# Layer 1 of a two-layer decoder: one compressor input for both block halves, its key part moved ahead of the last keys, and scores of both query tiles issued together

## The chip, the cores and the metric

The kernel runs on one core of one Trainium2 chip. The metric is the device time of one execution in microseconds (us). "Before" is the median of three runs; the profile is of one more execution.

## What is computed

The reference is a decoder trunk of two layers on 256 tokens of width 1024 in fp32. Layer 0 mixes tokens by stick-breaking and differential attention, layer 1 by a sparse attention with three branches; each mixer is followed by an MLP of width 4096. The change touches the mixer of layer 1 alone. Cut to what matters there:

```
def compress(t, pos, w1, w2):          # t: 256 x 4 groups x 64; CMP_LEN 32, CMP_STRIDE 16
    chunks = t.reshape(B, 16, 16, G, Dh)
    blocks = concatenate([chunks[:, r:r + 15] for r in range(2)], axis=2) + pos
    return gelu(flat(blocks) @ w1) @ w2            # 15 blocks per group, flat width 32 * 64

def nsa_attention(...):                            # 16 heads in 4 groups, 256 queries in 2 tiles
    o_cmp = softmax(q kc^T - slope * distance) vc          # over the 15 compressed blocks
    o_sel = softmax(q ks^T - slope * distance) vs          # selected keys: all of the past here
    o_win = softmax(q kw^T - slope * distance) vw          # window keys: all of the past here
    return g0 * o_cmp + g1 * o_sel + g2 * o_win
```

A block of 32 tokens is two neighbouring chunks of 16. So the product with `w1` is one product for the first halves of the blocks (chunks 0 to 14) and one for the second halves (chunks 1 to 15).

## The kernel before

All projections are "split" products: each fp32 weight tile is cast to a high part by ScalarE (L66), its low part is subtracted out by VectorE (L69), and TensorE makes three products per 128 rows (high by high, high by low, low by high). `Weights` holds them: raw tiles come by DMA on SP's queue (4 half-tile buffers), split ones have 4 buffers, and `get` splits one tile ahead. The order of `weight_order` is the order in which they are taken.

`odd_mixer` writes the order of TensorE's work by hand. Its pieces are generators, and `run(a, b, ...)` interleaves their steps in proportion. A scheduling layer below then fixes every engine's queue and gives out the buffers. The pieces are:

- `keys("ks")`, `keys("kw")`: selected and window keys, 48 matmuls each (`ps_k`), copied to `kd` by ScalarE (L720) and VectorE (L721).
- `queries(g)`: 48 matmuls (`ps_q`) per group of four heads, evicted to `qs` by ScalarE (L950).
- `compress_blocks(kv)`: the compressor's input, keys (kv = 0) or values (kv = 1): 48 matmuls (`ps_c`), and a transposed position row (`ps_pos`). Copies on ScalarE (L877) and VectorE (L879) bring the result into two tiles `fsk` or `fsv`, one for the first and one for the second halves of the blocks: 8 copies on each engine, and a fill on GpSimd (L864). It also loads eight tiles of `w1` (`cwk`, `cwv`). All these tiles share one ring of 12 buffers (`small`), with the transposed probabilities `pT` of later.
- `compress_hidden(kv)`: 16 products `ps_h` of the `fs` and `cw` tiles; `compress_gelu`: copies `ps_h` out (`hc`, L897), transposes it and adds the position (`ps_hT`, by the matrix `fold`), and applies gelu on ScalarE and VectorE (L905 to L921); `compress_keys`, `compress_values`: the product with `w2` (`ps_co`).
- `nsa_scores(g, t, b)`: four products per group g, query tile t (128 keys for t = 0, 256 for t = 1) and branch b, into one of two PSUM buffers of the tag `s2`. VectorE then adds the distance and finds the extreme (L975), ScalarE exponentiates (L978), and GpSimd scales (L983). `nsa_cmp_scores(g)` (`sc`) takes one of the same two buffers.
- `nsa_transposes`, `nsa_products` (steps of `values`): transposes of the probabilities (`pt`), their copies `pT` on ScalarE and VectorE in turn (L1031, L1029), and the product with the values (`o`).

Apart from the scores, every PSUM result of these pieces takes one of four banks of the tag `B`, so a result that isn't copied out holds its bank. The hand-written order before is: keys ks, queries 0, keys kw with scores (0,0) between, compressor blocks of keys, then of values, half of queries 1, hidden of keys, the other half of queries 1, hidden of values, and so on.

## Time and profile before

| | |
|---|---|
| median of 3 runs | 662.26 us (661.87 to 663.5) |
| profiled execution | 662.43 us, its span 660.7 us |
| TensorE matmul busy | 641.3 us, 97% of the span |
| VectorE busy | 407.7 us |
| ScalarE busy | 345.5 us |
| GpSimd busy | 46.3 us |
| mean granted TensorE clock | 0.991 |

The span is the time from the first to the last instruction. The rest of the execution's time, 1.7 us, lies around it. A wait is put down to the releaser that came last. A matmul's row gives its start and the time until its result is out, which is longer than the distance to the next matmul's start, because matmuls overlap. An fp32 product of scores, transposes or the compressor shows as two records.

### The profile page before, as it was taken

The numbers are of one execution on the slowest core, as the hardware profiler recorded it, in microseconds if no ns is written. First come the engines' busy times: TensorE is split into PE (matmuls) and PEld (weight loads), VectorE is DVE, ScalarE is ACT, GpSimd is POOL, SyncE is SP. The second block draws the span as 40 slices with busy tenths as digits, with TensorE's granted clock in tenths as the row PEclk, the third lists the DMA queues.
The fourth block names the chain that finished last, engine by engine and source line by source line (L and its number), as shares of the span: only waits on it lengthen the run. The fifth ranks groups of instructions, "written<-read, shape, count | busy, mean of one in ns | idle before, by whom it ended". The sixth has DMA issues, their size and how long they took to land.

```text
span 660.7 us, 11136 instructions
## 1 busy us (share of the span) xinstructions
PE 641.3 (97%) x4257; PEld 562.2 (85%) x4257; DVE 407.7 (62%) x820; ACT 345.5 (52%) x699; POOL 46.3 (7%) x139
## 2 busy tenths in 40 slices
PE   6999999999999999999999899999999999999995
PEld 3799898899898989988899778777899898999984
DVE  4845577886555555555877476776765555555534
ACT  5564666464444444543567374654554444444523
POOL 2200000000000000000203231440000000000000
PEclk8899999999999999999999999999999999999999
DMA  6785243456565556664596612014365555555501
GB/s 253 226 257 157 73 176 106 156 183 208 178 182 182 186 188 192 191 191 141 173 307 208 223 64 64 23 43 156 118 214 186 182 183 181 188 189 189 192 2 64
DMA packets 74277, 108.67 MB, mean 164 GB/s; under 512 B 5072, under 2 KB 60400, under 8 KB 74224
## 3 DMA queue, kind: packets, MB, share of 16 engines
q1 hardware_dynamic: 74224, 107.97, 50.9%
q8 instruction: 33, 0.54, 0.3%
q14 instruction: 20, 0.16, 0.1%
HBM read 106.91 MB, written 1.05 MB: 163 GB/s over the span
## 4 chain that ended last, share of the span: by engine, by line
PE 90%; DVE 5%; ACT 2%; issue 1%; DMA 1%; SPq 0%; ACTq 0%; DVEq 0%
PE macc L108 27%; PE ps_up L108 24%; PE ps_f L108 7%; PE acc L108 5%; PE ps_q L108 4%; PE ps_ut L108 3%; PE ps_v L108 2%; PE o L108 2%; PE s L108 2%; PE ps_or L108 2%; PE ps_k L108 2%; PE pt L1026 2%; DVE wl L69 2%; PE z L108 1%; PE ps_h L108 1%
## 5 line engine op out<-in xcount | busy, mean ns | idle before, releaser
L69 DVE TENSOR_TENSOR wl<-w,wh 128x1024 fp32r<-128x1024 f32 (+1 forms) x188 | 224.9, 1214 | 166.1 <-ACT wh L66 165.6
L66 ACT CAST wh<-w 128x1024 fp32r<-128x1024 f32 (+1 forms) x190 | 192.9, 1040 | 172.7 <-PE macc L108 83.3
L108 PE MATMUL macc<-wh,l 128*128 128x512 f32 x256 | 101.2, 395 | 0.0
L108 PE MATMUL macc<-wh,h 128*128 128x512 f32 x256 | 101.1, 395 | 0.0
L108 PE MATMUL macc<-wl,h 128*128 128x512 f32 x256 | 101.0, 394 | 0.0
L108 PE MATMUL ps_up<-m0h,wh 128*128 128x256 f32 x224 | 63.5, 283 | 0.0
L108 PE MATMUL ps_up<-m1h,wh 128*128 128x256 f32 x224 | 63.5, 283 | 0.0
L108 PE MATMUL ps_up<-m0h,wl 128*128 128x256 f32 x224 | 63.4, 283 | 0.0
L108 PE MATMUL ps_up<-m1h,wl 128*128 128x256 f32 x224 | 63.3, 283 | 0.0
L108 PE MATMUL ps_up<-m1l,wh 128*128 128x256 f32 x224 | 63.3, 283 | 0.0
L108 PE MATMUL ps_up<-m0l,wh 128*128 128x256 f32 x224 | 63.3, 283 | 0.0
L108 PEld LDWEIGHTS macc<-wh,l 128*128 128x128 f32 x256 | 48.2, 188 | 11.1
L108 PEld LDWEIGHTS macc<-wh,h 128*128 128x128 f32 x256 | 48.4, 189 | 10.0
L108 PEld LDWEIGHTS macc<-wl,h 128*128 128x128 f32 x256 | 48.3, 189 | 10.0
L108 PEld LDWEIGHTS ps_up<-m0l,wh 128*128 128x128 f32 x224 | 42.9, 191 | 0.6
L108 PEld LDWEIGHTS ps_up<-m1l,wh 128*128 128x128 f32 x224 | 42.9, 191 | 0.6
L108 PEld LDWEIGHTS ps_up<-m1h,wh 128*128 128x128 f32 x224 | 42.9, 191 | 0.6
L108 PEld LDWEIGHTS ps_up<-m0h,wh 128*128 128x128 f32 x224 | 42.9, 191 | 0.6
L108 PEld LDWEIGHTS ps_up<-m1h,wl 128*128 128x128 f32 x224 | 42.9, 191 | 0.0
L108 PEld LDWEIGHTS ps_up<-m0h,wl 128*128 128x128 f32 x224 | 42.9, 191 | 0.0
L983 POOL TENSOR_SCALAR p<-p,sums 128x128 f32<-128x128 f32 (+1 forms) x64 | 31.4, 508 | 80.5 <-ACT kd L720 25.8
L108 PE MATMUL ps_f<-x0h,wh 128*128 128x256 f32 x128 | 36.5, 285 | 0.0
(285 smaller groups left out, 1191.2 us busy)
## 6 DMA issues: line engine op xcount, KB each, us to landing
w<-in_mlp_w_dram SPq DMA_DIRECT2D x128, 512.0 KB, 4.3
w<-in_ev_w_in_dram SPq DMA_DIRECT2D x24, 512.0 KB, 4.8
w<-in_od_w_in_dram SPq DMA_DIRECT2D x18, 512.0 KB, 5.0
w<-in_ev_w_out_dram SPq DMA_DIRECT2D x8, 512.0 KB, 4.3
w<-in_od_w_out_dram SPq DMA_DIRECT2D x8, 512.0 KB, 3.6
cwk<-in_od_cmp_k_w_dram SPq DMA_DIRECT2D x8, 256.0 KB, 6.5
cwv<-in_od_cmp_v_w_dram SPq DMA_DIRECT2D x8, 256.0 KB, 5.1
w<-in_od_w_in_dram SPq DMA_DIRECT2D x4, 304.0 KB, 2.9
```

Source lines behind the costliest of these rows:

```text
L66: self.nc.scalar.copy(wh[:, c], w)
L69: eng.tensor_sub(wl[:, c], w, wh[:, c].bitcast(F32))
L108: self.nc.tensor.matmul(out, lhsT, rhs, start=start, stop=stop, **kw)
L983: nc.gpsimd.tensor_scalar(o[:, h], o[:, h], sums[:, h : h + 1], 0.0, op0=ALU.mult, op1=ALU.add)
L1026: nc.tensor.transpose(pt[:, h * P : (h + 1) * P], p[g, t, b][:, h, kt * P : (kt + 1) * P], self.ident)
```

## The change

The input of the compressor is held in one tile `fs` of its own (66 columns per step: a position column, 64 chunk columns, a position column) and both halves of the blocks read it, shifted by two columns; it has 16 columns a group instead of 15, so the copies are 4 on each engine and each part, and GpSimd fills nothing. `fold` is moved to the new columns. The ring `small` has 11 buffers instead of 12. The compressor's key part (`compress_blocks(0)`) now stands ahead of the keys kw, its hidden product right behind them, and the value part follows; the loads are reordered to fit. The scores of the two query tiles are issued one behind the other, and their softmax behind both; in the `values` steps they follow the products.

```
@@ -229,8 +229,8 @@

         W.add(("ks",), cols(w, 1536, 256))
         q(0)
+        W.add(("c", 0), cols(w, 1024, 256))
         W.add(("kw",), cols(w, 2048, 256))
-        W.add(("c", 0), cols(w, 1024, 256))
         W.add(("c", 1), cols(w, 1280, 256))
         q(1)
         q(2)
@@ -730,67 +730,79 @@

             def scores(g, b):

-                yield 2
-                for t in range(2):
-                    self.nsa_scores(g, t, b, qs, kd, gates, p, up, banks)
+                todo = [self.nsa_scores(g, t, b, qs, kd, gates, p, up, banks) for t in range(2)]
+                for f in todo:
+                    next(f)
+                return todo
+
+            def cmp_scores(g):
+                todo = self.nsa_cmp_scores(g, qs, kd, gates, pc[g % 2], banks)
+                next(todo)
+                return [todo]
+
+            def soft(todo):
+                for f in todo:
+                    for _ in f:
+                        pass
+
+            def once(f, n=3):
+
+                yield n
+                for i in range(n):
+                    if i == n // 2:
+                        f()
                     yield 1

-            def cmp_scores(g):
-                self.nsa_cmp_scores(g, qs, kd, gates, pc[g % 2], banks)
-
             order = [(g, t) for g in range(NG) for t in range(2)]

-            def values(i):
+            def values(i, *scores):

                 g, t = order[i]
                 todo = self.nsa_transposes(g, t, p, pc[g % 2], parts, up)
                 yield next(todo)
                 for n, _ in enumerate(todo):
-                    if n == 0 and i > 0:
-                        products(i - 1)
+                    if n == 0:
+                        if i > 0:
+                            products(i - 1)
+                        for f in scores:
+                            soft(f())
                     yield 1

             def products(i):
                 g, t = order[i]
                 self.nsa_products(g, t, parts, oT, v2, vc)

+            f = [None, None]
             run(keys("ks", CW))
             run(queries(0))
-            run(keys("kw", CW + S), scores(0, 0))
-            f = [None, None]
-            run(self.compress_blocks(0, xT, up, pool, f), scores(0, 1))
-            run(self.compress_blocks(1, xT, up, pool, f))
-            q1 = queries(1)
-            next(q1)
-            run(part(q1, KT))
+            run(self.compress_blocks(0, xT, up, pool, f))
+            run(keys("kw", CW + S), once(lambda: soft(scores(0, 0))))
             h = [self.bankB(f"ps_h{kv}") for kv in range(2)]
             run(self.compress_hidden(f[0], h[0]))
             hk = self.compress_gelu(0, h[0], up)
-            run(part(q1, KT))
-            run(self.compress_hidden(f[1], h[1]), scores(1, 0))
+            run(self.compress_blocks(1, xT, up, pool, f))
+            run(queries(1), once(lambda: soft(scores(0, 1))))
+            run(self.compress_hidden(f[1], h[1]))
+            soft(scores(1, 0))
+            self.compress_keys(hk, f[0], kd)
             hv = self.compress_gelu(1, h[1], up)
-            self.compress_keys(hk, f[0], kd)
             q2 = queries(2)
             next(q2)
-            run(part(q2, KT), scores(1, 1))
+            run(part(q2, KT))
+            soft(cmp_scores(0))
+            soft(scores(1, 1))
             self.compress_values(hv, f[1], vc)
-            cmp_scores(0)
             run(part(q2, KT), values(0))
-            cmp_scores(1)
             q3 = queries(3)
             next(q3)


-            run(values(1), part(q3, 4))
-            run(values(2), part(q3, 6), scores(2, 0))
-            run(values(3), part(q3, 6), scores(2, 1))
-            cmp_scores(2)
+            run(values(1, lambda: cmp_scores(1)), part(q3, 4))
+            run(values(2, lambda: scores(2, 0)), part(q3, 6))
+            run(values(3, lambda: scores(2, 1)), part(q3, 6))
             rows = self.out_rows("odo", oT)
-            next(values4 := values(4))
-            run(part(values4, 1))
-            run(part(values4, 2), part(rows, 2), scores(3, 0))
-            run(values(5), part(rows, 2), scores(3, 1))
-            cmp_scores(3)
+            run(values(4, lambda: cmp_scores(2), lambda: scores(3, 0)), part(rows, 2))
+            run(values(5, lambda: cmp_scores(3), lambda: scores(3, 1)), part(rows, 2))
             run(values(6), part(rows, 2))
             run(values(7), part(rows, 2))
             products(7)
@@ -835,9 +847,10 @@
         return pool.tile(shape, F32, tag="p1", name=name, bufs=4)

     def small(self, pool, shape, name):
-        return pool.tile(shape, F32, tag="p2", name=name, bufs=12)
+        return pool.tile(shape, F32, tag="p2", name=name, bufs=11)

     def compress_blocks(self, kv, xT, up, pool, f):
+


         yield 2 * KT
@@ -857,26 +870,24 @@
                 w = self.small(up, [P, 2, S], f"cw{nm}{u}{hf}")
                 nc.sync.dma_start(w, w1[u, hf])
                 ws.append(w)
-        fs = [self.small(up, [P, 8, 64], f"fs{nm}{hf}") for hf in range(2)]
+        fs = up.tile([P, 8, 66], F32, tag="fs", name=f"fs{nm}", bufs=1)
         pp = self.bankB("ps_pos")
         nc.tensor.transpose(pp[:, :16], pos, self.ident[:16, :16])
         for hf in range(2):
-            nc.gpsimd.memset(fs[hf][:, :, 61:], 0.0)
-            nc.scalar.copy(fs[hf][:, :, 60], pp[:, 8 * hf : 8 * hf + 8])
+            nc.scalar.copy(fs[:, :, 65 * hf], pp[:, 8 * hf : 8 * hf + 8])
         w = self.W.get(("c", kv))
         for m in range(2):
             ps = self.bankB("ps_c")
             yield from self.fmajor_steps(ps[:, :S], w, m, xT)
             for i in range(2):
                 src = ps[64 * i : 64 * i + 64, :S].rearrange("p (n j r) -> p r j n", j=8, r=2)
-                for hf in range(2):
-                    for r in range(2):
-                        o = fs[hf][64 * r : 64 * r + 64, :, 15 * (2 * m + i) : 15 * (2 * m + i) + 15]
-                        z = src[:, r, :, hf : hf + 15]
-                        if r == 0:
-                            nc.scalar.copy(o, z)
-                        else:
-                            nc.vector.tensor_copy(o, z)
+                c = 1 + 16 * (2 * m + i)
+                for r in range(2):
+                    o = fs[64 * r : 64 * r + 64, :, c : c + 16]
+                    if r == 0:
+                        nc.scalar.copy(o, src[:, r])
+                    else:
+                        nc.vector.tensor_copy(o, src[:, r])
             yield 1
         f[kv] = fs, ws, w2
@@ -886,7 +897,7 @@
         fs, ws, _ = f
         for j in range(8):
             for hf in range(2):
-                self.mm(hp[64 * hf : 64 * hf + 64, :S], fs[hf][:, j, :], ws[2 * (j // 2) + hf][:, j % 2, :],
+                self.mm(hp[64 * hf : 64 * hf + 64, :S], fs[:, j, 2 * hf : 2 * hf + 64], ws[2 * (j // 2) + hf][:, j % 2, :],
                         j == 0, j == 7, skip_group_check=True)
             yield 1
...
@@ -925,8 +936,8 @@
     def compress_keys(self, hT, f, kd):
         po = self.bankB("ps_co")
         for i in range(2):
-            self.mm(po[:, :60], f[2][:, i, :], hT[:, i, :60], i == 0, i == 1)
-        self.nc.scalar.copy(kd[:, :, :15], po[:, :60].rearrange("p (g n) -> p g n", n=15))
+            self.mm(po[:, :64], f[2][:, i, :], hT[:, i, :], i == 0, i == 1)
+        self.nc.scalar.copy(kd[:, :, :15], po[:, :64].rearrange("p (g n) -> p g n", n=16)[:, :, :15])

     def compress_values(self, hT, f, vc):
         po = self.bankB("ps_co")
@@ -971,6 +982,7 @@
             d = slice(64 * (h % 2), 64 * (h % 2) + 64)
             self.mm(z[h], qs[g][d, h // 2, t * P : (t + 1) * P], kd[d, g, c0 : c0 + n], True, True,
                     skip_group_check=True)
+        yield 1
         for h in range(4):
             nc.vector.tensor_tensor_reduce(out=o[:, h], in0=z[h], in1=self.dist[:, 2 * P - n : 2 * P], op0=ALU.add,
                                            op1=ALU.min, scale=-self.slope(4 * g + h), scalar=BIG,
...
```

What the built program shows of this, on three places. The first is TensorE where the hidden product of the key part (`ps_h` from `cwk`, `fsk`) begins. Before, it stood behind half of queries 1:

```order
L108 MATMUL ps_q<-x1h,wl_4031 128x256
L108 MATMUL ps_h_4143<-cwk_3858,fsk_3874 64x256
L108 MATMUL ps_h_4143<-cwk_3860,fsk_3875 64x256
...
L108 MATMUL ps_h_4143<-cwk_3872,fsk_3875 64x256
L108 MATMUL s_4205<-kd,qs 128x128 x2
L108 MATMUL s_4235<-kd,qs 128x256
L108 MATMUL ps_hT<-fold,hc 128x64 x2
L108 MATMUL s_4235<-kd,qs 128x256
L108 MATMUL ps_q<-x1h,wh_4030 128x256
```

Now it stands behind the keys kw, and the value part's `ps_c` follows it:

```order
L108 MATMUL ps_k<-x1h,wl_3768 128x256
L108 MATMUL ps_h_3947<-cwk_3746,fsk 64x256
L108 MATMUL ps_h_3947<-cwk_3748,fsk 64x256
...
L108 MATMUL ps_h_3947<-cwk_3760,fsk 64x256
L108 MATMUL s_4104<-kd,qs 128x128 x3
L108 MATMUL ps_hT<-fold,hc 128x64 x2
L875 MATMUL ps_pos<-ident,pos 128x16
L108 MATMUL ps_c<-x1h,wh_3835 128x256
```

The key part's hidden product has moved ahead of all 48 matmuls of the value part and of queries 1. The second place is VectorE at the gelu of the value part (`gel`, then its result `hT`). Before:

```order
L907 TENSOR_SCALAR gel<-gel 128x128
...
L909 TENSOR_SCALAR gel<-gel 128x128
...
L910 RECIPROCAL gel<-gel 128x128
...
L921 TENSOR_TENSOR hT_4272<-ps_hT,gel 128x16x15
L921 TENSOR_TENSOR hT_4275<-ps_hT,gel 128x16x15
L980 RECIPROCAL sums<-sums 128x4
```

Now:

```order
L918 TENSOR_SCALAR gel<-gel 128x128
L992 RECIPROCAL sums<-sums 128x4
L993 TENSOR_TENSOR sums<-sums,gates 128x4
L920 TENSOR_SCALAR gel<-gel 128x128
L921 RECIPROCAL gel<-gel 128x128
L1011 TENSOR_TENSOR pc_3398<-sc_4297,dist 128x4x16
L932 TENSOR_TENSOR hT_4254<-ps_hT,gel 128x16x15
L932 TENSOR_TENSOR hT_4257<-ps_hT,gel 128x16x15
```

The reciprocal of `sums`, which needs all four exponentials of a score group, stands inside the gelu now, and the first add of the compressed scores ahead of `hT`. The third place is ScalarE at the scores of group 2 in the `values` steps. Before, a copy of transposed probabilities stood between the two score groups:

```order
L273 CAST o1h<-o_4626 128x2x128
L978 ACTIVATE p,sums<-p,nm 128x128 x4
L1031 COPY pT<-pt_4672 128x512
L978 ACTIVATE p,sums<-p,nm 128x256 x4
L950 ACTIVATE qs<-ps_q,qscale 128x256
L1031 COPY pT<-pt_4743 128x512
```

Now:

```order
L273 CAST o1h<-o_4604 128x2x128
L990 ACTIVATE p,sums<-p,nm 128x128 x4
L990 ACTIVATE p,sums<-p,nm 128x256 x4
L1044 COPY pT<-pt_4672 128x512
```

All eight exponentials of the two query tiles now stand ahead of the copy.

## Rows read from the trace of the kernel before

**Rows 1.** Page of the profile: span, busy time by engine, chain that ended last by engine.

```profile
span 660.7 us, 11136 instructions
...
PE 641.3 (97%) x4257; PEld 562.2 (85%) x4257; DVE 407.7 (62%) x820; ACT 345.5 (52%) x699; POOL 46.3 (7%) x139
...
PE 90%; DVE 5%; ACT 2%; issue 1%; DMA 1%; SPq 0%; ACTq 0%; DVEq 0%
```

**Rows 2.** Windows (us): length, busy by engine, PE clock, DMA share, GB/s.

```profile
361.00:397.00 36.00, 33.05 (x266) 28.44 (x266) 21.66 (x76) 21.20 (x70) 10.46 (x20) 1.00 0.40 135
...
397.00:450.00 53.00, 53.00 (x419) 40.18 (x418) 36.93 (x146) 29.02 (x93) 16.35 (x36) 1.00 0.17 51
```

**Rows 3.** Timeline of TensorE, 365.5 to 384 us: start, duration, instruction, [idle before].

```profile
366.72 0.28 PE L108 MATMUL ps_c<-x1l,wh 128*128 128x256 f32 x1
366.84 0.28 PE L108 MATMUL ps_c<-x1h,wl 128*128 128x256 f32 x1
367.51 0.36 PE L108 MATMUL ps_q<-x1h,wh 128*128 128x256 f32 x1 [0.39 <-DVE fsk L879]
...
370.34 0.28 PE L108 MATMUL ps_q<-x1h,wl 128*128 128x256 f32 x1
371.29 1.05 PE L108 MATMUL ps_h<-cwk,fsk 128*64 128x256 f32 x7 [0.67 <-issue]
...
376.42 0.70 PE L108 MATMUL s<-kd,qs 64*128 64x256 f32 x2
377.91 0.39 PE L108 MATMUL ps_q<-x1h,wh 128*128 128x256 f32 x1 [0.79 <-ACT fsv L865]
...
380.76 0.28 PE L108 MATMUL ps_q<-x1h,wl 128*128 128x256 f32 x1
381.18 0.62 PE L108 MATMUL ps_h<-cwv,fsv 128*64 128x256 f32 x2
382.72 0.93 PE L108 MATMUL s<-kd,qs 64*128 64x128 f32 x8 [0.92 <-ACT qs L950]
```

**Rows 4.** Tile fsv (duration ns min/median/max, first and last start); waits; ScalarE's timeline.

```profile
L865 ACT COPY fsv<-ps_pos x2: 153/164/175, 377.6 to 377.7; 128x8 f32<-128x8 f32 x2
...
POOL fsv L864 <- PE ps_h L108: 7.9, 1, 7.9
...
370.71 0.47 ACT L950 ACTIVATE qs<-ps_q,qscale 128x256 f32<-128x256 f32 x1 [1.62 <-PE ps_q L108]
```

**Rows 5.** Timeline of TensorE around two score groups.

```profile
344.68 0.28 PE L108 MATMUL ps_k<-x1h,wl 128*128 128x256 f32 x1
344.89 0.49 PE L108 MATMUL s<-kd,qs 64*128 64x128 f32 x4
345.31 0.39 PE L108 MATMUL ps_k<-x1h,wh 128*128 128x256 f32 x1
345.53 0.28 PE L108 MATMUL ps_k<-x1l,wh 128*128 128x256 f32 x1
...
417.09 0.72 PE L108 MATMUL s<-kd,qs 64*128 64x128 f32 x8
417.73 0.39 PE L108 MATMUL ps_q<-x1h,wh 128*128 128x256 f32 x1
```

**Rows 6.** Timelines of ScalarE and VectorE: gelu, one exponential, one weight cast.

```profile
376.52 0.28 ACT L905 ACTIVATE gel<-ps_hT 128x128 f32<-128x128 f32 x1 [1.07 <-PE ps_hT L108]
...
379.51 0.29 DVE L912 TENSOR_TENSOR gel<-ps_hT,gel 128x128 f32<-128x128 f32 x1
...
394.26 0.49 ACT L978 ACTIVATE p<-p,nm 128x256 f32<-128x256 f32 x1
...
380.96 1.04 ACT L66 CAST wh<-w 128x1024 fp32r<-128x1024 f32 x1
```

**Rows 7.** Tile cwv: DMA issues on SP's queue, and time from issue to landing.

```profile
L858 SPq DMA_DIRECT2D cwv<-in_od_cmp_v_w_dram x8: 379/460/1196, 345.2 to 375.7; - x8
...
DMA to landing us min/median/max: 4.4/5.1/6.5
```

More of the change, by code (lines that the diff above doesn't have):

```diff
@@ L818, in nsa_constants @@
         e = pool.tile([P, 1], F32, name="fold_e")
-        nc.vector.tensor_add(self.fold, self.ident[:, :64], self.ident[:, 64:])
-        nc.vector.tensor_add(e, self.ident[:, 60:61], self.ident[:, 124:125])
+        nc.vector.tensor_add(self.fold, self.ident[:, 1:65], self.ident[:, 64:])
+        nc.vector.tensor_add(e, self.ident[:, :1], self.ident[:, 127:])
         nc.vector.tensor_scalar(self.fold, self.fold, e, None, op0=ALU.add)
@@ L918, in compress_gelu @@
             nc.gpsimd.memset(o, 0.0)
-            xi, ei = (z[:, 64 * i : 64 * i + 60].rearrange("p (g n) -> p g n", n=15).unsqueeze(2)
+            xi, ei = (z[:, 64 * i : 64 * i + 64].rearrange("p (g n) -> p g n", n=16)[:, :, :15].unsqueeze(2)
                       .to_broadcast([P, NG, 4, 15]) for z in (x, e))
@@ L995, in nsa_cmp_scores @@
                             skip_group_check=True)
+        yield 1
         for t in range(2):
```

## The prediction, made before the changed kernel had run

> **What bounds the kernel now.** I read the page first. TensorE is busy for 641.3 of 660.7 us, and 90% of the chain that ended last runs over it [rows 1]. So a change pays only where it takes out time in which TensorE has nothing to issue, or makes it issue less. The second view is the windows [rows 2]: in 361 to 397 us TensorE is idle for 36.00 - 33.05 = 2.95 us by its own row, in 397 to 450 us for nothing. The clock is 1.00 in both, so it plays no part.
>
> That idle time is too small a measure. A plain 256-column matmul here lasts 0.28 us but the next one starts 0.12 us later (366.72 to 366.84), so a stall shorter than the overlap doesn't show as idle. The reader should go by starts. In [rows 3] four steps are longer than their work: 366.84 to 367.51, 370.34 to 371.29, 376.42 to 377.91 and 381.18 to 382.72. The Trainium skill (Perfetto Trace Analysis, Identifying the Most-Contended Engine) says the same in general: matmul busy time is no good measure of the headroom, and the busy share of the weight loads is to be used. By the matmul row this stretch could give back 2.95 us at most; by the weight loads' 28.44 of 36.00 us [rows 2] the room would be 7.56 us. My terms below come from the starts and lie between.
>
> The four stalls have one cause, which [rows 4] show. GpSimd's fill of the value part's input `fsv` waits 7.9 us for the hidden product of the key part. `fsv` lives in the ring of 12 buffers, where eight `cwk` tiles, two `fsk` and two `cwv` tiles leave no place. So the value part's position row and its two `ps_c` results stay in three of the four PSUM banks until 377.6 us, some 10 us after they were made (366.84 is the last of them). In between TensorE works with the one bank that is left: the hidden product at 371.29 starts as soon as the eviction of 370.71 (0.47 us long, so until 371.18) frees it, and the second half of queries 1 at 377.91 starts when the position row is out. The last stall, before the score group of 382.72, waits for an eviction by a ScalarE that is then catching up on the `fsv` copies.
>
> **The change part by part.**
>
> *The jam.* `fs` gets a buffer of its own, and it is free for the value part once the key part's hidden product is done, which now comes ahead of the value part. So its `ps_c` can be copied out at once. The four stalls lose: 367.51 - 366.84 - 0.12 = 0.55 us, of which 0.10 is what any switch of matmul shape costs (0.22 to the second `ps_k` after a score group instead of 0.12 [rows 5]), so 0.45; 371.29 - 370.34 - 0.12 = 0.83, of which 0.30 stays, the entry of the other hidden product (380.76 to 381.18), so 0.53; 377.91 - 376.42 = 1.49 less 0.27 for two score records and 0.10 for the switch, so 1.12; 382.72 - 381.18 = 1.54 less two steps of 0.12 and a 0.09 switch, so 1.21. Sum 3.3 us.
>
> *Fewer visits of score groups.* A visit costs more than its records [rows 5]: entry 344.68 to 344.89 is 0.21 instead of 0.12; four records last 0.42 and eight 0.64, so 0.055 per record and 0.20 per visit; the exit is 0.22 instead of 0.12. Together 0.09 + 0.20 + 0.10 = 0.39 us. Before, TensorE's queue has 25 separate visits of `s` and `sc` groups; now it has 17, 6 of the 8 saved ones by the end of the compressor. 8 x 0.39 = 3.1 us. Ends: nothing, if the groups that now follow each other wait for buffers, and 3.1.
>
> *The copies and fills.* Half of the copies into `fs` go, 8 on ScalarE and 8 on VectorE over both parts, and four fills on GpSimd. TensorE hides all of that; I cost it at nothing beyond the jam.
>
> *A new wait at the value part's `ps_co`.* Between the end of `ps_hT` and the first `ps_co` of the values TensorE now has 24 matmuls of queries 2 (2.88 us) and one visit with 16 records of `sc` and 8 of `s` (24 x 0.055 + 0.39 = 1.7 us), 4.6 us in all. The gelu alone took 376.52 to 379.80, 3.3 us [rows 6]. Now four exponentials of 256 columns (4 x 0.49 = 2.0 us) stand on ScalarE between its square and its exponential, with the reciprocal that waits for them inside the gelu on VectorE, and ScalarE reaches the square some 0.5 us late, behind the exponentials of 128 columns. That makes 5.8 - 4.6 = 1.1 to 1.2 us; I take 1.1. Ends: 0, if ScalarE is ahead, and 3.3, the whole gelu uncovered. Queued behind it on TensorE are the other `ps_co`, the scores (1,1) and the transposes.
>
> *The key part's `hc`.* On ScalarE two weight casts (1.04 us each [rows 6]) now stand between the copies of kw, ahead of `hc`, and the first can't start before the last matmul of kw has read the buffer that it overwrites. The hidden product covers most of it; I take 0.4 us, ends 0 and 1.0.
>
> *Two PSUM buffers for three score groups.* In the steps of groups 2 and 3 the third group waits until VectorE has read the first, and a copy of probabilities waits behind eight exponentials. I take 0.1 us at each of four places, 0.4; ends 0 and what the second rival says.
>
> *Loads.* SP's queue is reordered: the last five `cwv` loads wait for the key part's hidden product, as six do now, and land 4.4 to 6.5 us after issue [rows 7]. That product now ends at about 362 us, the loads have landed by about 369, and the hidden product of the values needs them some 13 us after the key part's has ended (48 `ps_c`, 48 `ps_q`, a score pair). I cost it at nothing, with 7 us to spare. The moved weight tile of the compressor's keys takes the place of an equal one.
>
> Sum: 3.3 + 3.1 - 1.1 - 0.4 - 0.4 = 4.5 us less. Against the profiled execution that is 662.43 - 4.5 = 657.9; its time lies 0.17 above the median of the runs shown, so against the median I say 657.8 us. Nothing behind the mixer changes, and TensorE is never idle there, so what is gained arrives at the end. The gain's ends: 6.4 if nothing new waits, and about 0.9 if the new waits cost 3.3, 1.0 and four times 0.3.
>
> **The rivals.**
>
> *The gelu's wait is long (chance 0.2).* ScalarE and VectorE fall behind in the stretch where two score pairs, a gelu and two weight tiles come together. For it speaks that both are in-order and the gelu now has foreign work inside; against it that ScalarE is busy for only 21.20 of 36.00 us there [rows 2]. Price: 3.3 instead of 1.1, so a gain of 2.3: 660.0 us. It decides from the point where ScalarE reaches the square more than 2 us late.
>
> *The jam only moves (0.06).* If the loads of `cwv`, or another buffer, hold the value part up as before, the 3.3 us stay and 1.2 us are gained: 661.1 us. The 7 us to spare speak against it.
>
> *Slower (0.07): copies behind bursts.* In four places (groups 2 and 3, both branches) the copies `pT` that a product needs now queue on ScalarE behind eight exponentials (up to 8 x 0.49 = 3.9 us [rows 6]) where before one stood between the two fours. TensorE covers that with its queries or output products, 15 to 18 matmuls of 0.12 us and some transposes, or 12 of the output's longer ones, 3 to 4 us. If the burst starts late, behind the eviction of the product before it, up to 2 us of each are exposed, 8 us in all: 662.3 - 4.5 + 8 = 665.8 us. It turns the sign from 1.1 us of exposure at each place. Against it: in 397 to 450 us, where the bursts already are with one copy between, TensorE was idle for nothing [rows 2].
>
> **How the numbers follow.** The forecast has 0.67. A measurement of this kernel can tell about 0.3%, 2.0 us. Faster by more than that: all of the forecast except its lowest corner, 0.65, and three quarters of the first rival, 0.15, in all 0.8. Within 0.3%: the rest of both and the second rival, 0.13. Slower: 0.07. The range runs from 655.9 (nothing new waits, 6.4) to 661.2, which takes in both milder rivals and the forecast's low end; the slower rival is left out.
>
> **What would show it.** Right, if after the change `fs` of the values is written within a few us of its `ps_c`, no TensorE step between the hidden product of keys and that of values exceeds 0.6 us beyond its work, and the first `ps_co` of the values shows a wait of about 1 us on VectorE. The stretch from the first compressor matmul to the first transposes would be 4 us shorter, and the rest of the mixer about 0.5. Wrong, if `ps_co` waits 3 us, if `ps_h` of the values waits for a DMA, or if products wait for `pT` on ScalarE in the groups 2 and 3.

## The result, and the profile after

The changed kernel takes **659.24 us** (median, 657.15 to 661.65) against 662.88 us of the kernel before on the same chip: ratio 0.9943, 95% interval 0.9921 to 0.9964, so 2.4 to 5.2 us faster. A second comparison gave 657.90 us and 0.9917 (0.9905 to 0.9929). The forecast was 657.8 us in a range from 655.9 to 661.2, a gain of 4.5 us.

The page of the profiled execution after (657.15 us, its fastest), beside [rows 1]:

```profile
span 655.4 us, 11124 instructions
...
PE 636.0 (97%) x4257; PEld 559.1 (85%) x4257; DVE 403.6 (62%) x812; ACT 344.1 (52%) x691; POOL 45.0 (7%) x135
...
PE 90%; DVE 4%; ACT 3%; issue 1%; DMA 1%; SPq 0%; ACTq 0%; DVEq 0%
```

TensorE makes the same 4257 matmuls as before. What fell is their time, and nothing else bounds the kernel.

To see where it fell I measure two lengths from starts on TensorE. The **stretch** goes from the last matmul of queries 0 (its start plus 0.12 us) to the first matmul of queries 3; it holds the compressor. The **values stage** goes on from there to the first matmul behind the mixer (`acc`). Both together are called the mixer here; they hold the same work before and after. Windows with these bounds, first of before, then of after (columns as in [rows 2]):

```profile
344.44:403.70 59.26, 56.31 (x457) 48.47 (x456) 39.35 (x137) 37.88 (x117) 18.04 (x36) 1.00 0.47 153
403.70:455.42 51.72, 51.72 (x393) 38.62 (x391) 36.20 (x137) 29.57 (x93) 14.47 (x32) 1.00 0.18 55
```

```profile
343.80:397.89 54.09, 52.40 (x457) 45.93 (x456) 35.75 (x125) 35.95 (x110) 17.07 (x34) 1.00 0.50 161
397.89:450.14 52.25, 51.85 (x393) 38.86 (x391) 35.77 (x140) 29.88 (x92) 14.24 (x32) 1.00 0.18 55
```

The stretch lost 5.17 us, the values stage gained 0.53, so the mixer lost 4.64 (110.98 to 106.34). From the mixer's end to the span's end it is 205.28 us before and 205.26 after: what the mixer gives arrives whole. The span fell by 5.3 because the mixer of this execution also began 0.6 us earlier, which the change has no part in; in the second profile of the changed kernel (mixer 106.44) it began 1.0 us later than before. One execution's time differs from the next by some 2 us. The mixer's length differed by 0.1 us between the two profiles of the changed kernel and between two of the best kernel below, all at a granted clock of 1.00, so the readings below go by the mixer and the times only confirm them.

TensorE's waits after, in the mixer (waiter, releaser, us in all, times, longest). Before there were four, of 0.9, 0.8, 0.7 and 0.4 us, which [rows 3] show:

```profile
PE ps_co L108 <- PE s L108: 0.9, 1, 0.9
PE ps_hT L108 <- ACT hc L908: 0.8, 1, 0.8
PE pt L1039 <- DVE pT L1042: 0.2, 1, 0.2
```

All four are gone and three new ones have come. The two larger ones in the timelines: TensorE,

```profile
361.07 0.71 PE L108 MATMUL s<-kd,qs 64*128 64x128 f32 x6
362.58 0.66 PE L108 MATMUL ps_hT<-fold,hc 128*128 128x64 f32 x4 [0.81 <-ACT hc L908]
...
386.49 0.69 PE L108 MATMUL s<-kd,qs 64*128 64x128 f32 x8
388.06 0.41 PE L108 MATMUL ps_co<-w2v,hT 128*128 128x64 f32 x2 [0.88 <-PE s L108]
```

ScalarE,

```profile
357.64 0.49 ACT L990 ACTIVATE p<-p,nm 128x256 f32<-128x256 f32 x1
...
360.25 1.04 ACT L66 CAST wh<-w 128x1024 fp32r<-128x1024 f32 x1
361.77 0.37 ACT L720 COPY kd<-ps_k 64x256 f32<-64x256 f32 x1 [0.47 <-DVE kd L721]
362.16 0.37 ACT L908 COPY hc<-ps_h 128x256 f32<-128x256 f32 x1
...
366.51 0.27 ACT L888 COPY fsv<-ps_c 64x128 f32<-64x128 f32 x1 [2.03 <-PE ps_c L108]
...
385.25 0.50 ACT L990 ACTIVATE p<-p,nm 128x256 f32<-128x256 f32 x1
385.75 0.30 ACT L919 ACTIVATE gel<-gel 128x128 f32<-128x128 f32 x1
```

and VectorE:

```profile
385.95 0.18 DVE L992 RECIPROCAL sums<-sums 128x4 f32<-128x4 f32 x1 [0.34 <-POOL p L995]
...
386.50 0.95 DVE L921 RECIPROCAL gel<-gel 128x128 f32<-128x128 f32 x1
387.37 0.16 DVE L1011 TENSOR_TENSOR pc<-sc,dist 128x64 f32<-128x64 f32 x1
387.56 0.72 DVE L932 TENSOR_TENSOR hT<-ps_hT,gel 128x240 f32<-128x240 f32 x2
```

The score group behind the keys' hidden product starts at 361.07, but `hc` is copied at 362.16, behind two weight casts and the last copy of kw, and the fold waits for it. Ahead of these stand the eight exponentials of the grouped scores, the last at 357.64; the first copy of kw follows at 358.25. The value part's `ps_co` is put down to a score group, but what it needs is `hT`, whose first tile is made from 387.56 on; ahead of it on VectorE stand the reciprocal of `sums`, the gelu's own reciprocal and an add of the compressed scores, and on ScalarE the gelu's exponential stands behind four exponentials, the last of which ends at 385.75. The value part's input is copied from 366.51 on, directly when its `ps_c` is done, where [rows 4] had 377.6.

The third wait is recorded with 0.2 us, but by starts there are three such steps in the values stage. Behind a query matmul the next one usually starts after 0.12 us; here a transpose (`pt` or `ptc`) starts 0.49 us after the matmul of 409.18, 0.34 after that of 416.29 and 0.41 after that of 417.03, 0.9 us too much in all. TensorE, then ScalarE and VectorE:

```profile
409.18 0.28 PE L108 MATMUL ps_q<-x1h,wl 128*128 128x256 f32 x1
409.67 0.66 PE L1039 MATMUL pt<-ident,p 128*128 128x128 f32 x4 [0.21 <-DVE pT L1042]
...
417.44 0.63 PE L1039 MATMUL pt<-ident,p 128*128 128x128 f32 x4
```

```profile
416.24 0.49 ACT L990 ACTIVATE p<-p,nm 128x256 f32<-128x256 f32 x1
416.74 0.56 ACT L1044 COPY pT<-pt 128x512 f32<-128x512 f32 x1
...
408.58 0.42 DVE L987 CUSTOM_DVE_ANT_0 p<-s,dist 128x256 f32<-128x256 f32 x1
408.92 0.69 DVE L1042 COPY pT<-pt 128x512 f32<-128x512 f32 x1
```

Each of these transposes starts within 0.15 us of the end of a copy `pT`, and the copy stands behind the adds or exponentials of a pair of score groups. The list of waits names `pT` for the first; for the other two it is read from these times. The kernel before has no such step above 0.26 us.

### The profile page after: what moved, and what is told of

Read it like the earlier page. It is cut to its first block, busy times and chain, and to the rows that moved or that the text cites. A ratio compares the mean times of both kernels' runs of the same rounds, so it can differ in the third digit from the quotient of the medians.

```text
span 655.4 us, 11124 instructions
## 1 busy us (share of the span) xinstructions
PE 636.0 (97%) x4257; PEld 559.1 (85%) x4257; DVE 403.6 (62%) x812; ACT 344.1 (52%) x691; POOL 45.0 (7%) x135
## 3 DMA queue, kind: packets, MB, share of 16 engines
HBM read 106.91 MB, written 1.05 MB: 165 GB/s over the span
## 4 chain that ended last, share of the span: by engine, by line
PE 90%; DVE 4%; ACT 3%; issue 1%; DMA 1%; SPq 0%; ACTq 0%; DVEq 0%
PE macc L108 27%; PE ps_up L108 25%; PE ps_f L108 7%; PE acc L108 5%; PE ps_q L108 3%; PE ps_ut L108 3%; PE ps_v L108 2%; PE o L108 2%; PE ps_or L108 2%; PE ps_c L108 2%; PE ps_k L108 2%; PE s L108 2%; PE pt L1039 1%; PE z L108 1%; DVE xg L294 1%
## 5 line engine op out<-in xcount | busy, mean ns | idle before, releaser
L108 PE MATMUL ps_f<-x0l,wh 128*128 128x256 f32 x128 | 36.2, 283 | 0.0
```

Of the source, the lines that this page charges most:

```text
L108: self.nc.tensor.matmul(out, lhsT, rhs, start=start, stop=stop, **kw)
```

## The experiments

Times are medians; each ratio is to the kernel before in the same comparison, where its median was between 662.14 and 663.70 us. Stretch, mixer and the visits of score groups (in the stretch + in the values stage) come from each run's profile.

| kernel | time, us | ratio, 95% interval | stretch | mixer | visits |
|---|---|---|---|---|---|
| before | 662.26 | 1 | 59.26 | 110.98 | 13 + 12 |
| after | 659.24 | 0.9943 (0.9921 to 0.9964) | 54.09 | 106.34 | 7 + 10 |
| after, again | 657.90 | 0.9917 (0.9905 to 0.9929) | 54.15 | 106.44 | 7 + 10 |
| once, one buffer, old order | 659.53 | 0.9959 (0.9941 to 0.9976) | 55.90 | 107.96 | 11 + 13 |
| once, two buffers, old order | 657.83 | 0.9934 (0.9921 to 0.9946) | 56.43 | 108.15 | 10 + 12 |
| the same, again | 659.30 | 0.9959 (0.9940 to 0.9978) | 54.86 | 106.58 | 10 + 12 |
| once, one buffer, copies twice | 661.73 | 0.9986 (0.9971 to 1.0001) | 57.68 | 109.74 | 11 + 13 |
| grouped scores alone | 667.79 | 1.0081 (1.0065 to 1.0097) | 63.69 | 116.13 | 7 + 10 |
| once + grouped, old order | 659.91 | 0.9948 (0.9934 to 0.9961) | 56.33 | 107.98 | 7 + 10 |
| once + new order, old scores | 658.69 | 0.9950 (0.9937 to 0.9963) | 55.69 | 107.38 | 12 + 12 |
| after, value product later | 656.77 | 0.9900 (0.9883 to 0.9917) | 53.95 | 105.35 | 7 + 8 |
| after, product and fold later | 655.22 | 0.9887 (0.9869 to 0.9905) | 52.63 | 104.04 | 6 + 8 |
| the same, again | 654.87 | 0.9891 (0.9872 to 0.9911) | 52.60 | 103.96 | 6 + 8 |
| the same, old scores | 657.29 | 0.9932 (0.9906 to 0.9958) | 54.60 | 106.07 | 12 + 11 |

**The input held once, old order, one buffer.** The edits of `fs`, `fold` and the shifted reads as in the change, nothing of its order or scores:

```
-        fs = [self.small(up, [P, 8, 64], f"fs{nm}{hf}") for hf in range(2)]
+        fs = up.tile([P, 8, 66], F32, tag="fs", name=f"fs{nm}", bufs=1)
```

> The kernel before with the compressor input held once in one buffer and a ring of 11, as in the change, but the old order of work and the old scores. Theory: the value part's input still has to wait for the hidden product of keys, so the jam stays: 59.3 us for the stretch, within 0.5 less one visit of 0.39; time as before within 0.3%. Rival: halving the copies is what helps, then 2 us or more come off.

It misses: 3.02 us of the mixer go (3.36 of the stretch) although the single buffer is freed for the values no earlier in the program than before, by the end of the keys' hidden product. One of the four stalls is left, and a new wait of 0.5 us stands ahead of the value part's fold. The stretch has 11 visits instead of 13 as well, some 0.8 us at the price found below; the expectation had counted one. TensorE and ScalarE of this run:

```profile
370.10 2.16 PE L108 MATMUL ps_h<-cwk,fsk 128*64 128x256 f32 x18 [0.62 <-ACT qs L949]
```

```profile
373.85 0.24 ACT L865 COPY fsv<-ps_pos 128x8 f32<-128x8 f32 x2 [3.80 <-PE ps_h L108]
...
374.69 0.43 ACT L876 COPY fsv<-ps_c 64x128 f32<-64x128 f32 x2
375.41 0.28 ACT L904 ACTIVATE gel<-ps_hT 128x128 f32<-128x128 f32 x1 [0.29 <-PE ps_hT L108]
```

ScalarE makes all its copies into `fsv` before the gelu, from 373.85 to 375.1 us, right behind the hidden product. In the kernel before they stood behind the gelu's square of 376.52 [rows 6] and on VectorE behind the gelu's reciprocal, and there were twice as many:

```profile
378.02 0.95 DVE L910 RECIPROCAL gel<-gel 128x128 f32<-128x128 f32 x1
379.01 0.47 DVE L879 COPY fsv<-ps_c 64x120 f32<-64x120 f32 x2
```

So the buffer was one part of the delay at most. What was left after the buffer had come free, the gelu and a double set of copies, is another.

**The same with each copy made twice**, to part the number of copies from their place:

```
-                    if r == 0:
-                        nc.scalar.copy(o, src[:, r])
-                    else:
-                        nc.vector.tensor_copy(o, src[:, r])
+                    for _ in range(2):
+                        if r == 0:
+                            nc.scalar.copy(o, src[:, r])
+                        else:
+                            nc.vector.tensor_copy(o, src[:, r])
```

> The kernel that only holds the input once, in the old order and with the old scores, with each copy into the input made twice: as many copies on ScalarE and VectorE as before, but no fill on GpSimd, and the value part's copies still ahead of its gelu on ScalarE. If the number of copies made the jam (theory A), the stalls come back, and the stretch rises from 55.9 to 58 to 59 us (59.3 before). If it was that the copies stood behind the gelu and the fill (theory B), the stretch stays within 0.8 us of 55.9.

57.68 us lies between the two: 1.78 of the 3.36 us come back. The largest piece is the first stall of [rows 3], now longer (1.05 us instead of 0.39), and the rows of VectorE say why: the copies of the key part's input stand between the low parts of weight casts.

```profile
364.85 0.28 PE L108 MATMUL ps_c<-x1h,wl 128*128 128x256 f32 x1
366.19 0.36 PE L108 MATMUL ps_q<-x1h,wh 128*128 128x256 f32 x1 [1.05 <-DVE fsk L879]
```

```profile
363.24 1.23 DVE L69 TENSOR_TENSOR wl<-w,wh 128x1024 fp32r<-128x1024 f32 x1
...
365.42 0.62 DVE L879 COPY fsk<-ps_c 64x128 f32<-64x128 f32 x2 [0.64 <-ACT fsk L877]
```

The number of copies is worth about half of what holding the input once gives, though this run loses it in part at another place than the kernel before. Of the other half some 0.8 us are the two visits. About as much is left for the place of the copies and the fills that are gone; these two were not parted from each other.

**Two buffers, old order.** `bufs=2` for `fs`, the ring at 10, `fold_e` in another pool to make room.

> The kernel before in its old order, with the compressor input held once per part, in two buffers, and a ring of 10: the value part's input can be written at once, the scores stay tile by tile (22 separate visits instead of 25). The stretch is from TensorE's first matmul behind queries 0 to its first matmul of queries 3: 59.3 us before, 54.0 us in the changed kernel. Theory (jam 3.3, visits 0.39 each): 59.3 - 3.3 - 1.2 = 54.8 us, and a time 4 to 4.5 us under before. Rival A (the jam is the whole gain): 54.0. Rival B (only the fewer visits gain): 58.1.

Its first profile gave 56.43 us, with a lower granted clock in a part of it. The same kernel a second time:

> The kernel that holds the input once in two buffers, in the old order, a second time for a second profile, since the first profile was of its slowest run. Expected: the stretch 55.2 to 55.9 us with no step of TensorE more than 0.6 us beyond its work between the two hidden products; the time 658 us. If the second buffer is worth nothing (rival), the stretch equals that with one buffer (55.9).

Windows, first profile, then the second:

```profile
394.00:396.00 2.00, 2.00 (x20) 2.00 (x18) 1.85 (x11) 0.00 (x0) 1.68 (x3) 1.00 0.00 0
396.00:398.00 2.00, 2.00 (x12) 2.00 (x11) 0.32 (x2) 1.40 (x4) 0.69 (x2) 0.52 0.00 0
398.00:400.00 2.00, 2.00 (x13) 2.00 (x13) 1.10 (x4) 0.44 (x2) 0.00 (x0) 0.63 0.00 0
```

```profile
396.00:400.00 4.00, 4.00 (x37) 3.54 (x37) 3.00 (x11) 2.49 (x6) 0.00 (x0) 1.00 0.02 4
```

At 1.00 the stretch is 54.86 and the mixer 106.58 us, below the range expected of the repeat and close to the 54.8 of the first theory (jam and three visits). No wait of [rows 3] is left between the two hidden products; the keys' one starts without a recorded wait at 371.06, and a wait of 0.5 us stands ahead of the value part's fold, as with one buffer. So two buffers give another 1.4 us of the mixer over one, with two visits fewer (22 against 24). By time the two can't be told apart (0.9934 and 0.9959 against 0.9959). **This kernel's mixer is as short as that of the whole change (106.34 and 106.44)**, in the old order and with the old scores.

**Grouped scores alone**, with the compressor as before: `scores`, `cmp_scores`, `values` and the two `yield 1` of the change, and in the order of work the calls that go with them, such as

```
-            run(self.compress_blocks(0, xT, up, pool, f), scores(0, 1))
+            run(self.compress_blocks(0, xT, up, pool, f), once(lambda: soft(scores(0, 1))))
```

> The old compressor, in its old order and with two input tiles in the ring of 12, and the new scores (both tiles together, 17 visits). Theory: the jam stays, the stretch loses six visits of 0.39, 59.3 - 2.3 = 57.0 us. Rival A (jam is all): 59.3. Rival B (visits are all): 54.0.

The stretch is 4.4 us longer, not 2.3 shorter; the three later stalls of [rows 3] stay, and instead of the first there is a larger one, earlier. TensorE, ScalarE and VectorE:

```profile
368.53 0.55 PE L108 MATMUL ps_c<-x1h,wh 128*128 128x256 f32 x1 [4.12 <-DVE fsk L894]
```

```profile
362.47 0.49 ACT L994 ACTIVATE p<-p,nm 128x256 f32<-128x256 f32 x1
```

```profile
363.09 0.18 DVE L996 RECIPROCAL sums<-sums 128x4 f32<-128x4 f32 x1 [1.40 <-ACT p L994]
...
366.09 1.34 DVE L69 TENSOR_TENSOR wl<-w,wh 128x1024 fp32r<-128x1024 f32 x1
367.47 1.20 DVE L894 COPY fsk<-ps_c 64x120 f32<-64x120 f32 x4
```

The copies that free `ps_c` stand behind eight exponentials on ScalarE and behind the reciprocal that waits for the last of them on VectorE, then between weight casts. This is the mechanism of the forecast's slower rival (copies behind bursts), at the compressor's input instead of the products.

Not all of the 5.2 us by which the mixer grows is the queue. During this wait the granted clock fell to half (366.9 to 373.7 us), and the 24 matmuls behind the wait ran at 1.2 instead of 2.4 GHz:

```profile
368.50:373.70 5.20, 5.17 (x24) 5.20 (x25) 0.46 (x2) 0.26 (x1) 0.00 (x0) 0.50 0.35 104
```

They took 5.2 us where 24 steps of 0.12 are 2.9. At 1.00 this mixer would be some 2.3 us shorter, an estimate from these rows, and still 2.9 us longer than before. The fastest of this kernel's six executions took 665.95 us, 3.3 more than the median of the kernel before (662.67).

**Grouped scores with the input held once, old order:** both edits together.

> The kernel before with the input held once (one buffer) and the grouped scores, in the old order of the compressor. The grouped scores alone in the old order cost 5.1 us; with the input held once half of the copies that queued behind the scores' work are gone. If the queue of copies is what made them dear (theory), most of the 5.1 us goes and the time is within 1.5 us of the kernel that only holds the input once (659.5 us). If the old order itself is what grouped scores do not bear (rival: the key part's copies lie behind the burst wherever they are few or many), it stays 3 us or more above it, near 663 to 665 us.

The first theory holds: 107.98 us, as without grouping (107.96). The same `ps_c` waits 1.67 us instead of 4.12; that, a wait of 0.74 us at the value part's `ps_co` and longer steps ahead of `pt` eat what the fewer visits give:

```profile
364.31 0.35 PE L108 MATMUL ps_c<-x1h,wh 128*128 128x256 f32 x1 [1.67 <-DVE fsk L893]
```

**New order and input held once, scores tile by tile:** the change without its edits of `scores`, `cmp_scores`, `values`.

> The changed compressor in the changed order, with the scores tile by tile and spread over the steps as before (24 visits instead of 17). Theory: the jam is gone and the visits are back, 54.0 + 6 x 0.39 = 56.3 us for the stretch. Rival A (jam is all): 54.0. Rival B (visits are all): 59.

The stretch of 55.69 us lies nearer the theory than either rival, and the mixer of 107.38 us says that the new order gives 0.6 us over the old one with the same single buffer. Against this run the whole change is 1.0 us shorter, 1.6 less in the stretch and 0.6 more in the values stage. With the order in place grouping pays, but net a third of what was forecast, because it brings waits: without it the fold of the keys waits 0.3 us instead of 0.8, `ps_co` not at all, and no transpose in the values stage starts more than 0.26 us behind a query matmul.

**The two waits taken out.** First the value product behind the second half of queries 2:

```
-            self.compress_values(hv, f[1], vc)
             run(part(q2, KT), values(0))
+            self.compress_values(hv, f[1], vc)
```

> The changed kernel a second time, for a second profile and for times beside those of the three kernels that follow. Expected: the time within 1 us of its first median (659.2 us), the stretch from the end of the first queries to the first step of the fourth queries within 0.5 us of 54.1 us, with the two waits of the first profile back: about 0.9 us before the first step of ps_co of the values and about 0.8 us before the hT step of the keys.

> The changed kernel with the compressor's value product issued after the second half of the third queries and the first value group instead of ahead of them. If the wait of 0.88 us before ps_co is time that TensorE really loses (the theory of the prediction's third term), the wait goes and the stretch falls from 54.1 to about 53.2 us, the time by about 0.9 us. If the wait only stands in front of another one (rival: the products of the first group then wait for vc, or the first group's transposes for the same VectorE queue), the stretch stays within 0.3 us of 54.1.

Then also the key part's `hc` and fold, four steps into the value part's blocks:

```
-            hk = self.compress_gelu(0, h[0], up)
-            run(self.compress_blocks(1, xT, up, pool, f))
+            c1 = self.compress_blocks(1, xT, up, pool, f)
+            next(c1)
+            run(part(c1, 4))
+            hk = self.compress_gelu(0, h[0], up)
+            for _ in c1:
+                pass
```

> As the one before, and the key part's hc copy and fold step issued four steps into the value part's blocks, so that the copy has been made when the fold is reached. If the wait of 0.81 us before ps_hT is lost time, the stretch falls by another 0.8 us to about 52.4 us, and the time is about 1.7 us under that of the changed kernel. If the wait only passes on to ps_c of the values or to the copies of their input, the stretch stays near that of the run before (53.2).

> The kernel with both moves a second time, beside the run with tile-by-tile scores. Expected: 655.2 us within 1 us, ratio to before 0.988 to 0.990, mixer from the end of the first queries to the first step behind it 104.0 us within 0.4.

The repeat of the changed kernel has its two waits again (0.91 and 0.83 us). Its time missed the range set for it by 0.3 us. With the value product moved, the wait at `ps_co` is gone, the mixer is 1.0 us shorter and the time 1.1 (657.90 to 656.77 in one comparison, with intervals that overlap). But the stretch falls by only 0.2, so by the mark set beforehand the rival came true: the wait passes on, to a step of 0.65 us ahead of the score group at 389.19 and one of 0.41 ahead of the `ptc` at 393.11. The rest comes in the values stage, where the same work takes 51.40 instead of 52.25 us with 8 visits instead of 10. So the 1.0 us is not the price of the wait alone. With the fold moved too another 1.3 us go, a wait of 0.8 and one visit. That kernel's windows as above, and all waits of TensorE in the mixer:

```profile
343.76:396.36 52.60, 52.04 (x458) 45.58 (x456) 35.65 (x125) 36.41 (x110) 18.08 (x34) 1.00 0.54 170
396.36:447.72 51.36, 50.75 (x394) 38.33 (x392) 35.78 (x140) 29.47 (x91) 14.16 (x32) 1.00 0.15 49
```

```profile
PE pt L1043 <- DVE pT L1046: 0.4, 1, 0.4
PE ptc L1052 <- DVE pc L1032: 0.4, 1, 0.4
```

**It beats both kernels:** 0.9887 (0.9869 to 0.9905) and 0.9891 (0.9872 to 0.9911) of the time before, some 7.3 us, and its interval ends where that of the changed kernel in the same comparison begins (0.9905 to 0.9929).

**The same with scores tile by tile**, to price the visits where nothing else waits:

> The kernel with both moves (value product and fold issued later), but with the scores tile by tile as before: 23 visits on TensorE instead of 14 or 15. With the waits gone nothing hides the visits any more. If a visit costs 0.39 us as the prediction had it (theory), the mixer from the end of the first queries to the first step behind it is 8 x 0.39 = 3.1 us longer than with grouped scores (104.0 us), about 107.1, and the time about 3 us above that kernel's 655.2 us. If grouping pays only in the compressor's stretch and loses in the values stage (rival, from the comparison without the moves: -1.6 and +0.5 us), it is 105.0 to 105.5 us.

106.07 against 103.96 us, 2.1 us, and 657.29 against 654.87 in time: between the two cases. The stretch differs by 2.00 us, with 12 visits against 6 in its trace, 0.33 for each; the values stage by 0.11, with 11 against 8.

These figures are net. In the tile-by-tile run no transpose starts more than 0.26 us behind a query matmul, and TensorE has no recorded wait in the mixer. In the grouped kernel four of these steps are longer, where 0.12 is usual: 0.71 us in the stretch (from 390.41), and 0.72, 0.32 and 0.41 in the values stage (from 406.53, 413.88 and 414.61). With their excess put back, six visits are worth 2.00 + 0.59 = 2.59 us and three are worth 0.11 + 1.09 = 1.20, so 0.43 and 0.40 each. That is an estimate from these rows, and it is the price forecast in both stages. Kernels without grouping agree that visits cost in the values stage too: with 13, 12 and 11 of them it takes 52.05 (one buffer, old order), 51.72 (before) and 51.48 us (this run).

## Why the prediction was right, and where it was not

The sum was 4.5 us, the mixer gave 4.6 in the profiled execution and 4.5 in the second, and the two ratios say 3.8 and 5.5 us. That it agrees so closely is partly luck. The waits that the change brings cost more than forecast, 0.9 + 0.8 + 0.9 = 2.6 us instead of 1.9; with the visits at their price, by this estimate 4.6 - 3.1 + 2.6 = 4.1 us are left for the jam, the copies and the order, where 3.3 was forecast. The two errors offset each other, and the cause given for the largest term was only a part of it.

- **The jam (3.3 us).** The size is about right: holding the input once, alone, gives 3.4 us of the stretch, with two buffers 4.4, of which the fewer visits there (11 and 10 instead of 13) are some 0.8 and 1.2. The reason that the four stalls have one cause, no place for `fsv`, fails. The first of the four was never about `fsv`: its row names `fsk` on VectorE [rows 3], and doubling the copies brings that stall back with 1.05 us. Of the other three two go with one buffer that comes free at the same event as before. The number of copies, their place against the gelu and the buffer all count. The prediction costed the halved copies "at nothing beyond the jam", which was the wrong side of the account: in the old order they are the larger part of what one buffer gives, 1.8 of some 2.6 us without the visits. In the new order this was not parted.
- **Fewer visits (3.1 us).** Count and price hold: 25 visits before and 17 after, and some 0.4 us each, measured against the best kernel, where 0.39 was forecast. Net they give less, 2.1 us for nine visits in the best kernel and 1.0 for seven in the changed one, because grouping brings most of the waits that the next three terms are about.
- **The wait at the value part's `ps_co` (1.1 us).** 0.88 and 0.91 us, by the chain that was named: exponentials on ScalarE inside the gelu, reciprocal on VectorE, and a compressed-score add ahead of `hT`. The rival of a long wait (3.3) is refuted. What taking it out gives by itself is open.
- **The key part's `hc` (0.4 us).** It waited 0.81 us. Two weight casts between the copies of kw were foreseen, the eight exponentials ahead of them were not; with scores tile by tile the wait is 0.3 us. One of the prediction's signs fails here: between the two hidden products the step from the last score record (361.50) to the fold (362.58) is 1.08 us, more than 0.6 beyond its work.
- **PSUM and `pT` in groups 2 and 3 (0.4 us).** This is the term most under-sized: 0.9 us, in three steps ahead of transposes that wait for copies `pT` behind a pair of score groups. The values stage became 0.5 us longer where 0.5 shorter was forecast.
- **Loads.** No wait of TensorE in the mixer ends with a DMA. The 7 us to spare were enough.
- **The slower rival (0.07)** did not come, but its mechanism is real. At the place that it named it cost those 0.9 us, not up to 2 us at each of four places. With the compressor as it was, copies behind the same bursts held TensorE for 4.1 us at the compressor's input and made the kernel slower by 0.8%, a part of it through the clock. The change is faster because its other half had taken these copies out of the way.
- **The range.** By its own working the forecast's low end is 662.3 - 0.9 = 661.4 us, not 661.2; nothing hangs on it.

On the measure: before, TensorE's matmul row was idle in the mixer for 110.98 - 108.03 = 2.95 us (the two windows of before above). The best kernel took 7.0 us out of it with the same number of matmuls, and only 1.8 of these show as idle time of that row (103.96 - 102.79 = 1.17 us are left). The Trainium skill (Perfetto Trace Analysis, Identifying the Most-Contended Engine) holds the busy time of matmuls a bad measure of headroom, and this case agrees: by the weight loads' row the room was 110.98 - 87.09 = 23.9 us.

## What to carry to other kernels

Before a stall is put down to a missing buffer, read what stands between the event that frees the buffer and the instruction that uses it, in the queue of each engine: here a gelu and a double set of small copies. Grouping small matmuls saves TensorE's switches, some 0.4 us each here, and it turns the work behind them into a burst. The evictions that stand behind the burst then cost something back: 0.9 us in three steps of which the list of waits shows only one, and 4.1 us at one place where many copies stood there, with a fall of the clock on top. So make those evictions few or early first, and look for lost time by the steps between starts. Moving the consumer of a new wait some steps later can pass the wait on to the next one; the two moves here still gave 2.4 us, half as much again as the change, three visits fewer included.

## What was not expected of the hardware

- A score group of two records holds TensorE from its start to the next matmul for 0.42 us, as long as one of four did before (344.89 to 345.31) [rows 5], so the price per record plus a fixed visit, drawn from groups of four and eight, does not reach down to two.

```profile
400.38 0.48 PE L108 MATMUL s<-kd,qs 64*128 64x128 f32 x2
400.80 0.66 PE L1039 MATMUL pt<-ident,p 128*128 128x128 f32 x4
```

  The starts suggest why. In the group of four the records come in pairs 0.01 us apart (344.89 and 344.90, 345.10 and 345.11), in the group of two they come one by one (400.38, 400.60). The kernel puts the heads of a group alternately on the lower and the upper 64 partitions, and a visit with one head has no partner. No run tested this.
- Twice the granted clock fell to half inside the mixer. With the grouped scores alone it fell at 366.9 us, while TensorE had waited since its last matmul of 364.13, and it was back at 1.00 at 373.7, with TensorE busy again from 368.53 on. In the first profile with two buffers it was 0.52 and 0.63 in two windows of 2 us, so mostly at 1.2 instead of 2.4 GHz, with TensorE's matmuls and weight loads busy for the whole 2 us ahead of them; its work from 392.11 us on was mostly narrow products, `sc` of 16 columns and `ps_co` of 64, as it was in the other profile. The mixer was 1.6 us longer than in that kernel's other profile, where the same work ran at 1.00. What set the second fall off the runs don't show.
